# Stores of rotated queries and keys from GpSimd's DMA queue instead of SyncE's

## The chip, the cores and the metric

The kernel runs on one core of a Trainium2 chip. The metric is the device time of one launch in microseconds (us), the median of several runs. The core's engines are named TensorE (PE; PEld is its weight load), VectorE (DVE), ScalarE (ACT), GpSimd (POOL) and SyncE (SP); SyncE does no arithmetic here and only issues DMAs.

## The reference, cut to what matters

The reference is a transformer of two layers on 1024 main tokens and 256 context tokens, with a model dimension of 1024. Layer 0 has an attention mixer (a window attention with grouped keys and a differential attention over all tokens), layer 1 a gated linear attention; each is followed by a convolutional feed-forward network. Both are modulated by six vectors per layer, which are the products of a condition row with a large table. The part that matters here is the input of layer 0's attention: the normed tokens are projected to queries, keys and values, and the queries and keys of the main tokens are rotated by position.

```
aq, ak, av, bq, bk, bv = split(xn @ w_in)           # cn @ w_in for the context, not rotated
aq, ak, bq, bk = (apply_rope(t, cos, sin) for t in (aq, ak, bq, bk))
# apply_rope: x1, x2 = x[..., 0::2], x[..., 1::2]
#             even channels: x1 * c - x2 * s, odd channels: x1 * s + x2 * c
mod = silu(c) @ mod_w[layer] + mod_b[layer]          # six vectors: shift, scale, gate, twice
```

## The kernel before, in words

All operands are 32 bits wide. Every operand of a large product is split into a high part `hi` and a rest `lo`, and a product is three matmuls (hi by hi, hi by lo, lo by hi). `split` (L89) makes a pair of them: ScalarE copies the source to `hi`, then VectorE subtracts it from the source to give `lo`. Weights come in chunks of 512 KB through `load_w` (L95): a DMA into one of two buffers `wraw`, then a split into `whi` and `wlo` (three buffers each).

The stage of the change is `attn_in` (L292). It norms the tokens to `x1h` and `x1l`, and then runs fourteen projections (`part`, which calls `proj`, L103): each loads a weight chunk and multiplies it with all 1280 tokens, in two pieces of 512 columns and one of 256, eight chunks of the contraction deep and three matmuls each, into one of two PSUM buffers `big`. Six times two projections make a head pair (`pair`, L360): the even channels E of four heads and the odd ones O. VectorE multiplies the main tokens of both with cosine and sine (`ec`, `es`, `os`, `oc`, 1024 columns each), subtracts and adds, and the results are split into `shi` and `slo`, two buffers of each name; the 256 context columns are split straight from PSUM. Then the four results of the pair (hi and lo of the even and of the odd channels, 128 rows by 1280 columns, 640 KB each) are stored to a scratch in device memory: `qs` for the queries (pairs 0 to 3), `ks` for the keys (pairs 4 and 5). The scratch lies as [4 heads, 128 rows, 1280 tokens]; a store writes 32 rows of each head, `scr[:, r:r + 32, :]`. The two key heads of the window attention come from a projection of their own, in four stores of 320 KB (L405). The values are projected with the tokens as the stationary operand (`proj_tok`, L421, its matmuls at L434, 256 columns each), one half after the fourth pair and the other at the end of the stage.

In between, `some_mod` steps through the products of the condition rows with the modulation table, as work that VectorE does on the side: 48 blocks here, six after each pair and a few with the values. A block (`mod_block`, L247) is a DMA of 512 KB into one of two buffers `mraw` and two reducing products on VectorE (`junk` and `mraw`, with a short accumulator read).

The order of the work on each engine is laid down by the framework before the run: each engine has one list of instructions, and an instruction waits for semaphores at the head of its engine's list. In this stage no order is written out by hand. All DMAs of the stage, the loads of weights, table blocks and tables and also the stores, are issued from SyncE's list, by `dma` (L77). GpSimd's queue, by `dma2` (L80), is used for four DMAs late in the kernel; GpSimd does little else there (a few memsets). After the stage the attention reads the scratch back: ten keys of the context (`kc`), the queries (`q`, 120 DMAs) and ten keys of the main tokens (`km`), each load waiting for the stores that it reads from.

Of the kernel before, what the change touches and what calls it, by code (L numbers as in the profile page):

```python
# [9 lines left out]
F32 = mybir.dt.float32  # L10
# [8 lines left out]
P = 128  # L19
CC = 128                    # tokens of a chunk of the linear attention  # L20
KD = 8                      # chunks of the model dimension
NM = 1024                   # main tokens
NX = 256                    # context tokens
T = NM + NX
# [3 lines left out]
NB = 3                      # buffers of the norms  # L28
NFF = 22                    # chunks of the ffn dimension
# [5 lines left out]
class K:  # L35
    def __init__(self, nc, tc, io):
        self.nc, self.tc, self.io = nc, tc, io
        self.es = ExitStack()
        self.stacks = []
        self.urgent = False         # whether splits go before what was emitted earlier  # L40

    # ---------------------------------------------------------------- helpers
# [11 lines left out]
    def open_tmp(self, ny=2):  # L54
        """Room for the norms, on the right, until close_tmp."""
        self.es_tmp, self.ny = self.stack(), ny
        self.tmp = self.pool(self.es_tmp, "tmp", side="right")
# [22 lines left out]
    def dma2(self, out, in_):  # L80
        """On a queue of its own, for what would hold up the loads behind it."""
        return self.nc.gpsimd.dma_start(out, in_)

    def exp_tables(self, after):
        """Both Exp and Ln from one table set, until another function needs its own."""
        with self.tc.issue_after(after.ins):
            self.nc.scalar.preload_act_table_set("natural_log_exp_and_others")

    def split(self, hi, lo, src, urgent=False):  # L89
        """hi + lo = src: hi keeps 12 significant bits, lo the rest."""  # L90
        with self.tc.high_priority() if urgent else ExitStack():
            self.nc.scalar.copy(hi, src)  # L92
            self.tt(lo, src, hi.bitcast(F32), ALU.subtract)
# [8 lines left out]

    def proj(self, ps, w, xh, xl, tch, ks=range(KD)):  # L103
        """ps[:, t] += w^T x over the contraction chunks, weights stationary."""
        wh, wl = (a.rearrange("p (k n) -> p k n", k=KD) for a in w)
        for t0, n in tch:
            for k in ks:
                for j, (a, b) in enumerate(((wh, xh), (wh, xl), (wl, xh))):
                    self.nc.tensor.matmul(ps[:, t0:t0 + n], a[:, k, :], b(k, t0, n),  # L109
                                          start=(k == 0 and j == 0), stop=(k == KD - 1 and j == 2))  # L110

    def rstd_rows(self, hsrc, t0, n, on_pe=False):
        """1/sqrt(mean over the model dimension + eps), on every partition; on_pe: the squares are added up there."""
# [24 lines left out]
    def norm_mod(self, hsrc, xh, xl, t0, n, A, B, on_pe=False):  # L138
        """x = hsrc * rstd * A + B for tokens t0..t0+n, split in two."""
        y = self.rstd_rows(hsrc, t0, n, on_pe)  # L140
        for k in range(KD):
            self.norm_chunk(k, hsrc, xh, xl, t0, n, A, B, y)
# [8 lines left out]
    # ------------------------------------------------------------------ parts  # L151
    def setup(self):
# [23 lines left out]
        # per layer and norm: scale and shift of the normed rows, gate; [chunk, token kind]  # L176
# [4 lines left out]
        # scratch, in pieces that are written and read back each on its own  # L181
# [9 lines left out]
    def attn_consts(self, pool):  # L191
# [21 lines left out]
        # -lam  # L213
        self.stt(self.lam, ls[:, 1:2], -LAM_INIT, ls[:, 0:1], ALU.add, ALU.subtract)

    def mod_finish(self, l, j):
        """The j-th of the six vectors of layer l, once its products are there."""
# [15 lines left out]
    def mod_rows(self, pool, nv):  # L233
        """silu of the condition rows, on every partition."""
# [12 lines left out]
    def mod_block(self, pool, src, dst, rows):  # L247
        """dst[:, v] = block of the table, output rows on the partitions, times rows[v]."""
# [9 lines left out]
    def mod_first(self, pool, rows, load):  # L258
        """Shift and scale of the first norm: the one on the tensor engine, the other on the vector engine."""
# [24 lines left out]
    def mod_steps(self, todo, rows, pool):  # L284
        """The blocks of the vectors (l, j) of todo on the vector engine, one per step."""
# [8 lines left out]
    # -------------------------------------------------------- attention layer  # L294
    def attn_in(self, esv):
        nc, io = self.nc, self.io
        with ExitStack() as esx:
# [31 lines left out]
            with ExitStack() as es1:  # L329
# [27 lines left out]
                def pair(w0, scr):  # L357
                    """Four heads: their even channels, then their odd ones."""
                    def out(eo, t):
                        hi, lo = hl[eo]  # L360
                        self.split(hi[:, M], lo[:, M], t)
                        for half, y in ((0, hi), (1, lo)):
                            r = 64 * half + 32 * eo
                            self.dma(scr[:, r:r + 32, :], y.bitcast(F32))
# [26 lines left out]
                # the two key heads of the window attention: [even 0, even 1, odd 0, odd 1]  # L391
# [10 lines left out]
                for half, y in ((0, hi), (1, lo)):  # L402
                    for eo in range(2):
                        r = 64 * half + 32 * eo
                        self.dma(self.ks[2][:, r:r + 32, :], y[64 * eo:64 * eo + 64].bitcast(F32))  # L405
                some_mod(6)
                # values, token-major
# [13 lines left out]
    def proj_tok(self, srcs, fh, fl, dst, nblk):  # L421
        """256 columns, token-major: dst[b // per][:, b % per, :]."""
# [15 lines left out]
    def attn(self, fill, ahead):  # L438
        nc, io = self.nc, self.io
        with ExitStack() as es:  # L440
            es_k = es.enter_context(ExitStack())
            ap = self.pool(es, "attn")
            # keys: hi, lo on the rows; context and main tokens
# [29 lines left out]
            def scores(out, q, s, h, t0, n, mask=None):  # L473
                key = kc[h][:, t0 - NM:t0 - NM + n] if t0 >= NM else km[h][:, t0:t0 + n]
                nc.tensor.matmul(out, q[:, 0, s, :], key, start=True, stop=False)
                if mask is not None:
                    if n == 3 * P:
                        # the block in the middle is all in the window
# [8 lines left out]
            class Unit:  # L487
                """Shared by both kinds: the weights' transposes and their product with the values."""
# [29 lines left out]
            class UnitB(Unit):  # L518
# [20 lines left out]
                def w(self):  # L539
                    """p0 - lam (z0 / z1) p1, which still wants 1 / z0"""  # L540
# [83 lines left out]
            class CtxB(UnitB):  # L624
                """The two query blocks of the context; columns and sums by [block, map]."""
# [55 lines left out]
            class CtxA(UnitA):  # L681
                """Columns and sums by [block, head]."""
# [40 lines left out]
            def block_out(i, oc):  # L723
                """The block's outputs, transposed, to the scratch."""
# [31 lines left out]
            # A step takes one unit of either kind through its exponentials and  # L756
            # finishes the units of the step before.
# [61 lines left out]
    # ------------------------------------------------------ output projection  # L819
    def o_tiles(self, pool, name, n):  # L820
        """hi and lo of the mixer's outputs."""
# [4 lines left out]
    def halves_of(o, t0):  # L826
        """hi and lo as functions of chunk and tokens, which start at t0."""
        return [lambda k, a, b, t=t: t[k][:, a - t0:a - t0 + b] for t in o]

    def o_load(self, o, c, src, dma=None):  # L830
        """The split comes with the function that is returned."""
# [5 lines left out]
    def out_pass(self, wsrc, o, h, g, first=(), started=(), meanwhile={}):  # L837
        """h += gate * (w^T x) for the tokens of o, pairs of chunk and operands; started: sums that have the first pair."""
# [14 lines left out]
    # -------------------------------------------------------------------- ffn  # L853
    def ffn_first(self, l):
        """The first weights, ahead of the norm."""
# [6 lines left out]
    def ffn(self, l, fp, xh, xl, h, NT, first, in_order, last_norm, step, before_last, after_last, after):  # L862
# [8 lines left out]
        def load(group):  # L871
            """The group's chunks with their weights."""
            return [(self.load_w(io["ffn_down"][l, c]), a, b) for c, a, b in group]

        def down(group, order, after=None, urgent=False):
            """These chunks' part of the output, onto h."""
# [22 lines left out]
        # the first two projections begin while the last tokens are still being normed  # L899
# [51 lines left out]
    def body(self):  # L951
# [3 lines left out]
        with ExitStack() as esv:  # L955
# [6 lines left out]
            def begin():  # L962
                """The first output chunk of the projection, in between what ends the attention."""
# [19 lines left out]
        # output projection, norm2  # L983
# [30 lines left out]
        # ffn of layer 0, the condition's vectors of layer 1, then the first norm of layer 1  # L1014
# [79 lines left out]
        # gated linear attention  # L1094
# [42 lines left out]
    def gla_open(self, st):  # L1137
        """What the linear attention keeps throughout, at the right's bottom."""
# [7 lines left out]
        # the second gate product, its hi and lo parts stacked on the rows  # L1146
        self.w2 = [gp.tile([P, 512], F32R, name=f"w2s{d}") for d in range(2)]

    def gla_rst(self, rst, w, xh, xl, tch, off):
        """Low-rank gate rows: hi, lo, hi on rows 0, 32, 64 (+16) of rst[direction]; ones for the bias."""  # L1150
# [14 lines left out]
    def gla_ctx(self, st):  # L1165
        """The context's final states, either direction."""
# [44 lines left out]
    def gla_gates(self, pool, rst, h, d, n, L, b):  # L1211
        """b: running sums of 16 log a over each chunk (inclusive); L: the summands."""
# [17 lines left out]
    def gla_khat(self, k, b, be, n, m):  # L1230
        """k times the decay to the chunk's end (forward) and to its start (backward)."""
# [17 lines left out]
    def gla_decay(self, pool, b, bb, nch):  # L1249
        """exp of the chunk sums, [P, 2, nch]"""  # L1250
# [5 lines left out]
    def gla_update(self, dst, src, dec, kt, v):  # L1256
        """dst = dec * src + k^T v"""
# [7 lines left out]
    def gla(self, st):  # L1265
        nc, io = self.nc, self.io
        ch = self.ch
        with ExitStack() as es:
# [16 lines left out]
            for h in range(4):  # L1285
# [7 lines left out]
                # running sums: X inclusive (forward), exclusive (backward); I inclusive  # L1293
# [5 lines left out]
                # within a chunk: scores[s, t], from the diagonal outwards  # L1299
# [7 lines left out]
                for lev in range(7):  # L1307
# [5 lines left out]
                    # F[0]: decays that go with the keys, F[1]: with the queries  # L1313
# [17 lines left out]
                # across chunks  # L1331
# [13 lines left out]
                # states before each chunk, in either direction  # L1345
# [8 lines left out]
                # gate of the output  # L1354
# [8 lines left out]
                if h == 3:  # L1363
                    # the output projection's operands of the first tokens
# [12 lines left out]
                # outputs, token-major, normed over the head's columns  # L1377
# [35 lines left out]
# --------------------------------------------------------------------- layout  # L1413
def _chunks(w):
    """[1024, N] -> [N/128, 128 (rows in a chunk), 8 (row chunks) * 128]"""
# [4 lines left out]
def _cols(v):  # L1420
    """[..., 1024] -> [128, ..., 8]"""
# [4 lines left out]
def _wide(w):  # L1426
    """[1024, N] -> [N/256 * 2, 128, 4 * 256]: row chunks 0..3, then 4..7, of each 256 columns"""
# [5 lines left out]
def layout(x, c, ctx, c_ctx, mod_w, mod_b, norm1_g, norm2_g, attn_w_in, attn_w_out, attn_sink,  # L1433
# [17 lines left out]
    # rope tables: row p holds the angle of channel pair p % 32  # L1451
# [7 lines left out]
    # query and key columns: of four heads the even channels, then the odd ones  # L1459
# [14 lines left out]
    # window mask for the blocks before, at and after the query block  # L1474
# [50 lines left out]
```

## Time and profile before

| | us |
|---|---|
| median of the runs (3) | 3219.08 |
| lowest and highest run | 3217.68, 3223.64 |
| profiled execution: its span, first to last instruction | 3216.0 |
| busy in that span: TensorE | 3048.9 (95%) |
| busy: VectorE | 2026.6 (63%) |
| busy: ScalarE | 1142.7 (36%) |
| busy: GpSimd | 10.9 (0%) |

The page gives the span of the profiled execution and no other time for it; the runs' times contain what lies around the span as well. The shares are those of the whole kernel, an average over stages with different limits: what a change in one stage is worth has to be read in that stage. "Granted clock" is the share of TensorE's full speed; in the whole span it is 0.980. Waits are put down to the one of an instruction's semaphores that came last.

### The profile page before, as it was taken

To read this page: it belongs to the slowest core of one execution; us is meant where nothing else is said; L and a number is where in the kernel's file an instruction comes from. 1 tells how busy PE (TensorE), PEld (TensorE's weight loads), DVE (VectorE), ACT (ScalarE), POOL (GpSimd) and SP (SyncE) were. 2 spreads that over 40 slices of the span, in tenths; PEclk is the share of its full clock that TensorE was granted. 3 is DMA by queue.
4 is the path that set the end of the run, shared out by engine and by line. 5 is a ranking of instruction groups with operands and counts; after the bars stand their busy time and mean duration, and the time that the engine had idled before them with its cause. 6 is when DMAs were issued, how large, how long until landed. Compare 5 with 4: busy or idle time off the path is not lost. (4 is left out here: it accounts for less than half of the span.)

```text
span 3216.0 us, 40083 instructions
## 1 busy us (share of the span) xinstructions
PE 3048.9 (95%) x16390; PEld 2569.6 (80%) x16390; DVE 2026.6 (63%) x3124; ACT 1142.7 (36%) x1884; POOL 10.9 (0%) x22
## 2 busy tenths in 40 slices
PE   8768669999999999999999999999999999999998
PEld 4667569999887888888888878888877888888887
DVE  7566467888578744545455597688776554555546
ACT  5111147777443222222222264445354222221223
POOL 0000000000000000000000000000000000000000
PEclk9889789999999999999999999999999999999999
DMA  6434492221425311111111141111142111111111
GB/s 219 158 135 155 147 226 82 60 60 37 168 72 165 123 35 38 40 40 40 33 40 39 35 150 55 43 40 45 42 158 73 53 40 53 52 47 40 58 48 59
DMA packets 127831, 257.41 MB, mean 80 GB/s; under 512 B 11324, under 2 KB 70844, under 8 KB 127648
## 3 DMA queue, kind: packets, MB, share of 16 engines
q1 hardware_dynamic: 125600, 251.71, 23.9%
q8 instruction: 129, 2.11, 0.3%
q10 hardware_dynamic: 1728, 2.10, 0.2%
q0 software_dynamic: 320, 1.05, 0.1%
q14 instruction: 54, 0.44, 0.0%
HBM read 219.42 MB, written 35.39 MB: 79 GB/s over the span
## 5 line engine op out<-in xcount | busy, mean ns | idle before, releaser
L92 ACT CAST whi<-wraw 128x1024 fp32r<-128x1024 f32 x218 | 226.2, 1048 | 1202.3 <-PE big L109 641.9
L72 DVE TENSOR_TENSOR wlo<-wraw,whi 128x1024 fp32r<-128x1024 f32 x218 | 264.2, 1220 | 477.7 <-ACT whi L92 476.1
L109 PE MATMUL big<-x2h,whi 128*128 128x512 f32 (+1 forms) x1056 | 377.4, 357 | 1.8 <-ACT crow L75 1.2
L109 PE MATMUL big<-x2l,whi 128*128 128x512 f32 (+1 forms) x1056 | 377.0, 357 | 0.4 <-DVE x2l L69 0.3
L109 PE MATMUL big<-x2h,wlo 128*128 128x512 f32 (+1 forms) x1056 | 377.1, 357 | 0.0
L887 PE MATMUL sm<-gh,whi 128*128 128x512 f32 (+1 forms) x904 | 332.5, 368 | 3.0 <-DVE h L69 1.9
L887 PE MATMUL sm<-gl,whi 128*128 128x512 f32 (+1 forms) x904 | 329.3, 364 | 0.2 <-DVE gl L72 0.2
L887 PE MATMUL sm<-gh,wlo 128*128 128x512 f32 (+1 forms) x904 | 328.6, 364 | 0.0
L69 DVE SCALAR_TENSOR_TENSOR cv<-big,cw,cv 128x1023 f32<-128x1023 f32 (+1 forms) x264 | 267.1, 1012 | 21.0 <-ACT cv L75 17.7
L109 PE MATMUL big<-x4l,whi 128*128 128x512 f32 x704 | 277.7, 394 | 0.9 <-DVE x4l L69 0.9
L109 PE MATMUL big<-x4h,whi 128*128 128x512 f32 x704 | 276.7, 393 | 1.9 <-ACT x4h L75 1.9
L109 PE MATMUL big<-x4h,wlo 128*128 128x512 f32 x704 | 274.0, 389 | 0.0
L69 DVE SCALAR_TENSOR_TENSOR h<-sm,G,h 128x512 f32<-128x512 f32 (+1 forms) x280 | 179.8, 656 | 90.6 <-PE sm L887 89.9
L109 PEld LDWEIGHTS big<-x2h,whi 128*128 128x128 f32 x1056 | 198.8, 188 | 34.1 <-ACT crow L75 2.0
L109 PEld LDWEIGHTS big<-x2l,whi 128*128 128x128 f32 x1056 | 198.7, 188 | 32.5 <-DVE x2l L69 1.1
L109 PEld LDWEIGHTS big<-x2h,wlo 128*128 128x128 f32 x1056 | 198.6, 188 | 31.2
L887 PEld LDWEIGHTS sm<-gh,whi 128*128 128x128 f32 x904 | 170.3, 188 | 41.7 <-DVE h L69 7.4
L69 DVE SCALAR_TENSOR_TENSOR hh<-sm,G,hh 128x512 f32<-128x512 f32 (+1 forms) x192 | 137.5, 726 | 87.4 <-PE sm L887 87.1
L887 PEld LDWEIGHTS sm<-gh,wlo 128*128 128x128 f32 x904 | 170.3, 188 | 27.5 <-issue 0.2
L887 PEld LDWEIGHTS sm<-gl,whi 128*128 128x128 f32 x904 | 170.4, 189 | 26.6 <-DVE gl L72 0.6
L75 ACT ACTIVATE cv<-big,cb,cw 128x1024 f32<-128x1024 f32 (+1 forms) x132 | 130.6, 990 | 125.7 <-DVE cv L69 125.1
L109 PE MATMUL big<-x1h,whi 128*128 128x512 f32 (+1 forms) x336 | 125.3, 375 | 48.9 <-DVE slo L72 47.1
(348 smaller groups left out, 6141.4 us busy)
## 6 DMA issues: line engine op xcount, KB each, us to landing
mraw<-in_mod_wt_dram SPq DMA_DIRECT2D x88, 512.0 KB
wraw<-in_ffn_up_dram SPq DMA_DIRECT2D x88, 512.0 KB
wraw<-in_ffn_down_dram SPq DMA_DIRECT2D x44, 512.0 KB
q<-qs SPq DMA_DIRECT2D x40, 256.0 KB
q<-qs SPq DMA_DIRECT2D x80, 128.0 KB
wraw<-in_attn_w_out_dram SPq DMA_DIRECT2D x16, 512.0 KB
wraw<-in_gla_w_v_dram SPq DMA_DIRECT2D x16, 512.0 KB
wraw<-in_gla_w_out_dram SPq DMA_DIRECT2D x16, 512.0 KB
```

Source lines behind the costliest of these rows:

```text
L69: return self.nc.vector.scalar_tensor_tensor(out=out, in0=in0, scalar=scalar, in1=in1, op0=op0, op1=op1)
L72: return self.nc.vector.tensor_tensor(out=out, in0=a, in1=b, op=op)
L75: return self.nc.scalar.activation(out=out, in_=in_, func=func, **kw)
L92: self.nc.scalar.copy(hi, src)
L109: self.nc.tensor.matmul(ps[:, t0:t0 + n], a[:, k, :], b(k, t0, n), start=(k == 0 and j == 0), stop=(k == KD - 1 and j == 2))
L887: nc.tensor.matmul(o, w[:, d * P:(d + 1) * P], x[:, t0:t0 + n], start=(i == 0), stop=(i == 3 * len(group) - 1))
```

## The change

The 28 stores of rotated and split queries and keys to the scratch are issued from GpSimd's queue (`dma2`) instead of SyncE's (`dma`). Their sizes, sources, destinations and number stay, and so do all loads. The diff also drops comments and docstrings, line by line, so that line numbers stay; two lines of code differ:

```diff
@@ pair(w0, scr), out(eo, t) @@
                         self.split(hi[:, M], lo[:, M], t)
                         for half, y in ((0, hi), (1, lo)):
                             r = 64 * half + 32 * eo
-                            self.dma(scr[:, r:r + 32, :], y.bitcast(F32))
+                            self.dma2(scr[:, r:r + 32, :], y.bitcast(F32))
@@ the two key heads of the window attention @@
                 for half, y in ((0, hi), (1, lo)):
                     for eo in range(2):
                         r = 64 * half + 32 * eo
-                        self.dma(self.ks[2][:, r:r + 32, :], y[64 * eo:64 * eo + 64].bitcast(F32))
+                        self.dma2(self.ks[2][:, r:r + 32, :], y[64 * eo:64 * eo + 64].bitcast(F32))
```

## Rows read from the trace of the kernel before

**Rows 1.** The page: span.

```profile
span 3216.0 us, 40083 instructions
```

**Rows 2.** Timeline of SyncE: start, us, instruction; first store of some pairs.

```profile
88.32 0.69 SPq L78 DMA_DIRECT2D qs<-shi  x1
...
231.02 0.52 SPq L78 DMA_DIRECT2D qs<-shi  x1
...
308.27 0.52 SPq L78 DMA_DIRECT2D ks<-shi  x1
...
354.03 0.53 SPq L78 DMA_DIRECT2D ks<-shi  x1
```

**Rows 3.** Busy time by stretch, 60 to 428 us, sum of seven stretches.

```profile
sum 368.00, PE 267.41 PEld 233.03 DVE 215.59 ACT 54.59 POOL 0.00; mean PE 38.20 PEld 33.29 DVE 30.80 ACT 7.80 POOL 0.00
```

**Rows 4.** Waits of TensorE, 60 to 428 us: total us, times, longest.

```profile
PE big L109 <- DVE slo L72: 47.1, 7, 14.0
PE big L434 <- DVE slo L72: 16.5, 2, 15.9
PE big L434 <- DVE wlo L72: 14.5, 1, 14.5
PE big L109 <- DVE wlo L72: 12.7, 1, 12.7
```

**Rows 5.** Waits of VectorE, 60 to 428 us.

```profile
DVE junk L255 <- DMA mraw<-in_mod_wt_dram: 138.6, 17, 22.2
```

**Rows 6.** Timeline of VectorE, 148 to 171 us; in brackets idle before, releaser.

```profile
148.53 1.21 DVE L72 TENSOR_TENSOR es<-big,sin 128x1024 f32<-128x1024 f32 x1
149.66 1.21 DVE L72 TENSOR_TENSOR wlo<-wraw,whi 128x1024 fp32r<-128x1024 f32 x1
169.51 1.22 DVE L255 CUSTOM_DVE_ANT_0 junk<-mraw,crow 128x1024 bf16<-128x1024 f32 x1 [18.64 <-DMA mraw<-in_mod_wt_dram]
...
170.66 0.42 DVE L72 TENSOR_TENSOR slo<-big,shi 128x256 fp32r<-128x256 f32 x1
```

**Rows 7.** Timeline of SyncE, 142 to 158 us: DMA issues.

```profile
142.85 3.21 SPq L78 DMA_DIRECT2D qs<-slo  x1
146.16 7.43 SPq L78 DMA_DIRECT2D mraw<-in_mod_wt_dram  x2
153.64 4.74 SPq L78 DMA_DIRECT2D wraw<-in_w_v_dram  x2
```

**Rows 8.** DMA view, 139 to 172 us in 40 slices: busy share in tenths, GB/s.

```profile
DMA  0222132222222222479699838952222222222221
GB/s 0 50 50 62 74 107 68 99 99 99 99 93 99 112 112 99 125 215 400 243 389 395 359 149 191 385 223 106 106 112 99 106 99 81 84 104 104 104 109 79
```

**Rows 9.** DMA view of the whole span: one group of stores, KB each.

```profile
qs<-shi SPq DMA_DIRECT2D x8, 640.0 KB
```

**Rows 10.** Timeline of GpSimd, one of its four DMAs, and their landing (tile og).

```profile
2385.45 0.55 POOL L82 DMA_DIRECT2D oraw<-og  x1 [0.90 <-PE big L109]
DMA to landing us min/median/max: 2.3/3.3/7.2
```

**Rows 11.** Timeline of TensorE, 367 us: steps of 512 and of 256 columns.

```profile
367.17 0.40 PE L109 MATMUL big<-x1h,wlo 128*128 128x512 f32 x1
367.40 0.29 PE L109 MATMUL big<-x1h,whi 128*128 128x256 f32 x1
367.52 0.28 PE L109 MATMUL big<-x1l,whi 128*128 128x256 f32 x1
```

**Rows 12.** Timeline of VectorE, 419 to 426 us: one block of the table, two blocks on

```profile
419.77 1.23 DVE L255 CUSTOM_DVE_ANT_0 junk<-mraw,crow 128x1024 bf16<-128x1024 f32 x1 [0.98 <-DMA mraw<-in_mod_wt_dram]
...
425.74 1.23 DVE L255 CUSTOM_DVE_ANT_0 junk<-mraw,crow 128x1024 bf16<-128x1024 f32 x1 [0.91 <-DMA mraw<-in_mod_wt_dram]
```

**Rows 13.** Timeline of TensorE, 415 to 447 us: stage's last, attention's first.

```profile
418.78 0.28 PE L434 MATMUL big<-whi,x1l 128*128 128x256 f32 x1
432.69 0.55 PE L475 MATMUL big<-kc,q 128*128 128x256 f32 x1 [13.63 <-DMA q<-qs]
```

## The prediction

> **What bounds the kernel now.** I read the page first: the span is 3216.0 us [rows 1]. Then I looked for the stretch that the moved stores live in. The queue of SyncE shows the first of the four stores of each head pair starting at 88.32, 231.02, 308.27 and 354.03 us [rows 2]; the first three pairs are 142.7 us apart in all (47.6 each), the fourth, with one projection of the values in between, 77.3 us, the last 45.8 us. So this is the input stage of the attention, from about 60 to 428 us, and only there can the change act directly. The table by stretch says that TensorE is busy for 267.4 of these 368 us [rows 3]: 100 us are idle, in a kernel whose TensorE is otherwise the bound. The waits of TensorE name VectorE in four lines, 47.1 + 16.5 + 14.5 + 12.7 = 90.8 us [rows 4]. The waits of VectorE in turn name one thing: 138.6 us for blocks of the modulation table (mraw), 17 times, up to 22.2 us at a time [rows 5].
>
> One such wait, followed down: VectorE finishes a weight split at 150.9 us and then stands still for 18.64 us, until 169.51, for a block of mraw; behind it in its order is the split of the projection's context columns (slo from big), which is what frees the sum that TensorE needs [rows 6]. The loads it waits for were issued long before: SyncE issued the last of the four stores at 142.85, then two mraw blocks (from 146.16) and two weight blocks (from 153.64) [rows 7]. What holds them is seen in the DMA slices from 139 to 172 us, 0.825 us each: the busy share is 0.2 for the first 13 us, while only the stores move, at about 100 GB/s; then it is 0.5 to 0.9 for some 8 us, when the loads run; then it is 0.2 again until 171 us [rows 8]. A share of 0.2 to 0.25 is four of 16 engines. A pair has four stores of 640 KB [rows 9], 2.62 MB; at 105 GB/s that is 25 us, from 140 to 165. The loads finish on twelve engines in 8 us, and their share on the four, a quarter of 2.1 MB at 105 GB/s, 5 us, comes behind the stores: 165 + 5 = 170, where the wait ends. So the loads are late because on four engines they stand behind the stores.
>
> **The change, part by part.** It moves 28 stores (24 of 640 KB, 4 of 320 KB) to GpSimd's queue. Nothing is added or removed in the arithmetic. SyncE loses their issue and their waits: in one pair 3.3 us from the last store's issue to the next load's [rows 7]; taken alone this is hidden by the backlog above, and I count it at nothing beside it. GpSimd has nothing to do in this stretch (POOL busy 0 [rows 3]), so nothing queues behind a store that waits there for its split. Its price for a DMA stands in the only four that it issues today: 0.55 us busy, 1.45 us from one to the next, 2.3 to 7.2 us to landing for 256 KB [rows 10]. Four stores are issued in about 6 us of a pair of 30; it is hidden, and would cost only if it delayed the reuse of the split buffers by the next pair's first split, some 10 us after the stores.
>
> What the stores cost the loads then is not in the trace, since no store of this shape leaves from GpSimd. The one end: they spread over all engines. A pair moves 2.62 MB of stores and eight blocks of 512 KB, 6.8 MB in all; at 300 GB/s, which the mixed slices of [rows 8] reach (215 to 400), that is 23 us, less than either compute engine needs. The other end: they stay on the same four engines, only no longer ahead of the loads; then these four carry 25 us of stores and a quarter of 4.2 MB of loads, 10 us, 35 us a pair. I take the first, as the rows of GpSimd's own DMAs show 256 KB landed in as little as 2.3 us, which is 110 GB/s with the whole of issue and receipt in it, so that the moving alone was well above the 105 GB/s of four engines.
>
> With timely loads a pair costs:
> - TensorE: matmuls of 512 columns follow each other by 0.23 us, those of 256 by 0.12 [rows 11]. A projection has 48 and 24, 13.9 us; a pair 27.8; the values' projection has 240 of the short ones, 28.8.
> - VectorE: ten instructions of 1024 columns (six of the rotation, two splits, two weight splits) by 1.13 us [rows 6] are 11.3, two short splits 0.8, together 12.1. Six mraw blocks: at the stage's end, with no store in the way, two blocks take 5.97 us including a wait of 0.9 [rows 12], so six take 17.9. Some of these waits go where a block was fetched during the rotation; I take 17.3. Sum 29.4.
>
> So VectorE is next late, by little. I take 32 us a pair, 2.6 above this floor for the order between the two (VectorE's last blocks delay a freed sum). Between the pairs' stores: 5 x 32 + 28.8 = 189 us against 354.03 - 88.32 = 265.7, a gain of 77. After the last pair two projections, the transposes and the values' second half: from 354.03 to the last matmul of the stage at 418.78 [rows 13] 64.8 us pass; unhindered it is 6.4 to 13.9 for the first (TensorE has begun it before the last stores leave, or not), 13.9 for the second, 1 for the transposes and 28.8, about 54. A gain of 11. What follows, the start of the attention with its own loads, shifts as it is; I count no gain there. Sum: 88 us, so a span of 3216.0 - 88 = 3128. The median of the runs, 3219.08, is 3.1 above the profiled span; I take that as what lies around it and predict 3131.
>
> The bounds of this case: at the floor of 29.4 a pair, 5 x 29.4 + 28.8 = 176, a gain of 89, and 15 behind it (6.4 taken for the first projection), 104: 3115. At 36 a pair, 57 + 8 = 65: 3154.
>
> **The rivals.**
>
> *The stores keep their four engines.* Loads then pass them, but the four engines are busy for 35 us a pair, and the stores, stretched by the loads, hold the split buffers; the wait of VectorE for mraw is replaced by the one for the landing of a store. With 3 to 6 us of order on top a pair takes 38 to 41: 5 x 39.5 + 28.8 = 226, a gain of 40, and some 8 in the tail: 3171, from 3155 to 3190. For it: the shape of the transfer does not change, and the rows show this shape on four engines. Against it: the rate of GpSimd's DMAs above. [...]
>
> *Nothing to speak of.* The wait moves on: the two mraw buffers or the order that is laid down anew for the changed queues keep VectorE as late as now. For it: 0.9 us of wait for every second block stays without any store [rows 12]. Against: that is 3 us a pair, not the 18 to 22 of today. 3200 to 3222.
>
> *Slower: GpSimd can't issue fast enough.* The stores land so late that the next pair's splits wait for the buffers, and VectorE with them. The price: it decides from the point where four stores take longer than today's pair, 46 us, 11.5 us each, eight times the 1.45 us of [rows 10]; at 15 us each a pair takes 60, six pairs lose 84: 3303. For it: VectorE is busy nearly throughout a pair then, and the landing of 256 KB varied from 2.3 to 7.2 us. [...] Against: the factor of eight.
>
> **How the numbers follow.** Chances: the forecast 0.66 (3115 to 3154), four engines 0.20 (3155 to 3190), nothing to speak of 0.09, slower 0.05. The range from 3112 to 3182 holds nearly all of the first and most of the second, 0.8. Faster or slower by over 0.2% is 6.4 us, about what a measurement here can tell from no change. Faster takes the first two and half of the third, 0.91; within it 0.05; slower 0.04.
>
> **What would show it.** Right: the waits of VectorE for mraw fall from 138.6 to some 20 to 35 us, those of TensorE for VectorE from 90.8 below 25; pairs' stores on POOL about 32 us apart; the last matmul of the values near 331 us; no long plateau at a share of 0.2 that ends with a wait for mraw. Four engines: the plateau stays, VectorE waits for stores to land. Slower: issues on POOL many us apart. The forecast is wrong if the pairs' spacing falls and the stage's end does not, or if the attention behind it gives the gain back: its first score product starts 13.9 us after the stage's last matmul today [rows 13], and that gap should keep its length.

## The result and the profile after

The changed kernel takes 3164.11 us (median of four runs, 3162.18 to 3169.22) against 3218.38 us (four runs, 3216.29 to 3223.64): a ratio of 0.9833, interval 0.9819 to 0.9847. It is 54 us faster, of the 88 that were forecast. The time lies inside the range of the prediction and above its likeliest case (3115 to 3154).

The page gives the span and the busy times; those of TensorE and VectorE are the same as before to 0.3 us, so the gain is idle time.

```profile
span 3164.1 us, 40097 instructions
PE 3048.6 (96%) x16390; PEld 2570.0 (81%) x16390; DVE 2026.3 (64%) x3124; ACT 1142.1 (36%) x1884; POOL 29.9 (1%) x50
```

The timeline of GpSimd from 84 to 330 us, the first of the four stores of each of the six pairs and the rest of the first four; it answers to [rows 2].

```profile
87.35 0.86 POOL L82 DMA_DIRECT2D qs<-shi  x1 [86.89 <-ACT shi L92]
88.88 0.71 POOL L82 DMA_DIRECT2D qs<-slo  x1 [0.67 <-DVE slo L72]
89.58 0.68 POOL L82 DMA_DIRECT2D qs<-shi  x1
91.14 0.69 POOL L82 DMA_DIRECT2D qs<-slo  x1 [0.88 <-DVE slo L72]
132.36 0.68 POOL L82 DMA_DIRECT2D qs<-shi  x1 [40.53 <-ACT shi L92]
...
173.62 0.68 POOL L82 DMA_DIRECT2D qs<-shi  x1 [36.78 <-ACT shi L92]
...
214.12 0.68 POOL L82 DMA_DIRECT2D qs<-shi  x1 [36.03 <-ACT shi L92]
...
284.33 0.68 POOL L82 DMA_DIRECT2D ks<-shi  x1 [65.72 <-ACT shi L92]
...
323.37 0.68 POOL L82 DMA_DIRECT2D ks<-shi  x1 [34.56 <-ACT shi L92]
```

Pairs are 45.0, 41.3, 40.5 and 39.0 us apart, not 32, and 70.2 with the values in between. In all 323.37 - 87.35 = 236.0 us against 265.7: a gain of 29.7 where 77 were expected.

The waits of TensorE and VectorE in the same stage, now 60 to 380 us (total us, times, longest); they answer to [rows 4, 5].

```profile
PE big L109 <- DVE slo L72: 28.0, 7, 8.2
PE big L434 <- DVE slo L72: 13.4, 2, 10.1
PE big L434 <- DVE wlo L72: 7.9, 2, 7.7
PE big L109 <- DVE wlo L72: 6.0, 1, 6.0
DVE junk L255 <- DMA mraw<-in_mod_wt_dram: 92.8, 23, 13.7
```

TensorE's waits for VectorE fell from 90.8 to 55.3 us, VectorE's for the table from 138.6 to 92.8. It is the same chain of waits as before, with shorter links. A wait of TensorE can cost more than its length: after one of 6.4 us, up to 158.54, the granted clock is 0.50 until 163.80, and matmuls of 512 columns follow each other by 0.43 us there instead of 0.23.

The DMA view from 132 to 173 us, one pair, in 40 slices of 1.025 us; it answers to [rows 8]. The queue rows give packets, MB and the share of 16 engines (q0 is GpSimd's, q1 SyncE's).

```profile
DMA  0329799699699898799631100002938987850000
GB/s 0 36 45 176 214 227 165 154 215 245 225 334 295 304 293 297 237 234 340 260 141 73 55 33 28 0 0 52 308 152 256 316 280 200 276 208 0 0 0 0
q0 software_dynamic: 2112, 2.63, 29.0%
q1 hardware_dynamic: 1152, 4.19, 28.9%
```

The view of the tile mraw in the same stretch, six blocks:

```profile
DMA to landing us min/median/max: 3.1/9.0/17.3
```

The plateau at 0.2 is gone: the stores are on all 16 engines (at the peak some 16 of their packets of 5120 bytes move at once in the trace, mostly four before). But the engines are then 0.6 to 0.9 busy for some 17 us and move no more than 150 to 340 GB/s. The stores alone take 0.29 x 41 x 16 = 190 engine-us for 2.63 MB; before, four engines for some 25 us, 100. So the stores moved to four times the engines and cost almost twice the engine time, and a table block that goes out among them lands after up to 17.3 us.

The end of the stage and the start of the attention: TensorE, then SyncE's issues of after, SyncE's of before, and VectorE's of before. The TensorE rows answer to [rows 13].

```profile
380.44 0.28 PE L434 MATMUL big<-whi,x1l 128*128 128x256 f32 x1
380.56 0.28 PE L475 MATMUL big<-kc,q 128*128 128x256 f32 x1
...
368.82 0.33 SPq L78 DMA_DIRECT2D mraw<-in_mod_wt_dram  x1
...
369.77 4.91 SPq L78 DMA_DIRECT2D kc<-ks  x10
```

```profile
422.30 0.33 SPq L78 DMA_DIRECT2D mraw<-in_mod_wt_dram  x1
...
423.16 4.70 SPq L78 DMA_DIRECT2D kc<-ks  x10
...
413.88 1.22 DVE L255 CUSTOM_DVE_ANT_0 junk<-mraw,crow 128x1024 bf16<-128x1024 f32 x1 [20.83 <-DMA mraw<-in_mod_wt_dram]
```

The gap of 13.9 us between the two matmuls shrank to 0.1. Before, VectorE stood for 20.8 us at the stage's end for a late block; so it freed the buffers late, SyncE issued the last block only at 422.30, after TensorE's last matmul (418.78), and the attention's first loads stand behind that block in SyncE's list. Now they go out at 369.77, 11 us ahead of the stage's end. The whole gain up to the attention's first score product, 432.69 - 380.56 = 52.1 us, is then: first stores 1.0 earlier, pairs 29.7, tail after the last pair 64.8 - 57.1 = 7.7, start of the attention 13.8. The spans differ by 51.9, so almost nothing is given back later.

### The profile page after: what moved, and what is told of

Its sections match the earlier page's. It is cut to its first block, busy times and chain, and to the rows that moved or that the text cites. A ratio compares the mean times of both kernels' runs of the same rounds, so it can differ in the third digit from the quotient of the medians.

```text
span 3164.1 us, 40097 instructions
## 1 busy us (share of the span) xinstructions
PE 3048.6 (96%) x16390; PEld 2570.0 (81%) x16390; DVE 2026.3 (64%) x3124; ACT 1142.1 (36%) x1884; POOL 29.9 (1%) x50
## 2 busy tenths in 40 slices
DMA packets 139184, 257.46 MB, mean 81 GB/s; under 512 B 22676, under 2 KB 82196, under 8 KB 139000
## 3 DMA queue, kind: packets, MB, share of 16 engines
q1 hardware_dynamic: 122168, 234.67, 22.7%
## 5 line engine op out<-in xcount | busy, mean ns | idle before, releaser
L109 PEld LDWEIGHTS big<-x4h,whi 128*128 128x128 f32 x704 | 132.2, 188 | 34.1 <-ACT x4h L75 3.2
```

## The experiments

The theory after the result: what makes the loads late is how long, and on which engines, the stores hold the DMA engines; from GpSimd they use all 16 but crowd each other. Its rivals: four engines after all, with other packets between; the order laid down for the new queue; or a limit on writing as such. Beside these runs the kernel before had medians of 3218.7 to 3221.6 us.

**Stores alone (e5).** The network is replaced by groups of four stores, each group after the one before has landed:

```diff
+            for j in range(m):
+                q(s[:, 32 * j:32 * j + 32, :], src[j])
...
+        gate(); rows4(sy)
+        gate(); rows4(po)
+        gate(); rows4(ac)
...
+                for h in range(4):
+                    q(s[h, 32 * j:32 * j + 32, :], src[j][32 * h:32 * h + 32])
...
+                q(s[j], src[j])
```

> The whole network is left out; only groups of stores run, one group behind the other, with nothing beside them, and the output is filled with ones. Four stores of the kernel's form: from SyncE 25 us on four engines (share 0.25, 105 GB/s); from ScalarE the same four engines, 25 us; from GpSimd all 16 engines, four to a store. Theory 'crowded stores' (four stores on 16 engines slow each other, 5120-byte packets of 400 to 540 ns where one alone takes 196): 16 to 18 us at about 155 GB/s with no load near, while one store alone from GpSimd takes 7 us and two 7 to 9. Rival 'the loads beside them slow the stores': four from GpSimd alone take 7 to 9 us at 300 GB/s or more. If crowded: a limit on writing to device memory as such expects 155 GB/s for the head-by-head and the contiguous form too; a limit from the four stores reading the same rows of SBUF expects 300 GB/s and more for the head-by-head form (all engines on different rows) and no gain from a scratch for each store; a limit from the addresses in the scratch expects a gain from a scratch for each store.

The busy time by stretch, one stretch for each group, from where its first packets move (some 1.2 us behind the first issue) to its landing: us, busy times of VectorE and GpSimd, granted clock, share of 16 DMA engines, GB/s. In this order: the kernel's form from SyncE, GpSimd, ScalarE; one and two such stores from GpSimd; head by head from GpSimd; one whole contiguous block for each store from GpSimd.

```profile
9.20:36.30 27.10, 1.24 (x6) 0.00 (x0) 1.00 0.25 97
39.00:57.80 18.80, 1.24 (x6) 1.48 (x3) 1.00 0.69 140
60.00:88.00 28.00, 1.24 (x6) 0.00 (x0) 1.00 0.24 94
90.50:99.20 8.70, 0.00 (x0) 0.00 (x0) 1.00 0.25 76
102.30:115.30 13.00, 0.41 (x2) 0.15 (x1) 1.00 0.42 101
118.10:128.50 10.40, 1.24 (x6) 6.73 (x14) 1.00 0.84 252
...
143.40:150.20 6.80, 1.24 (x6) 1.11 (x3) 1.00 0.97 386
```

From SyncE or ScalarE the form keeps to a quarter of the engines (0.25 and 0.24) for 27 to 28 us. From GpSimd one store takes a quarter, two take 0.42, four 0.69, yet four need 18.8 us. The shares grow with the number of stores, so from GpSimd several at once are not held to one quarter. As engine time (us x share x 16) a store costs 27 from SyncE, 35 alone from GpSimd, 44 of two and 52 of four; why the one alone costs more than from SyncE stays open. The same bytes as contiguous blocks take 6.8 us at 386 GB/s: writing as such is no limit. One store and two were slower than expected (8.7 and 13.0 us for 7 and 7 to 9): already two disturb each other.

**No stores but the first pair's (e4).** The five other pairs and the window keys store nothing; all reads take the first scratch.

```diff
-                            self.dma2(scr[:, r:r + 32, :], y.bitcast(F32))
+                            if w0 == 0:
+                                self.dma2(scr[:, r:r + 32, :], y.bitcast(F32))
```

> The stores of all pairs but the first, and those of the window's keys, are left out, and all queries and keys are read from the first pair's scratch. Theory 'the stores still delay the loads': pairs 29 to 33 us apart (39 to 41 now), VectorE's waits for mraw in the stage under 40 us (92.8 now), time 3110 to 3130. Rival 'the loads' own buffers and order hold them': pairs 38 to 41 us apart, waits over 70 us, time 3150 to 3165.

One run: 3108.43 us, just under the theory's range. The casts of the odd sum, which mark the pairs, are 28.6, 28.7, 59.5 and 27.0 us apart from the second pair on. VectorE's wait for the table is left with this row of its waits from 60 to 300 us:

```profile
DVE junk L255 <- DMA mraw<-in_mod_wt_dram: 30.4, 15, 13.5
```

Up to the end of the stage it is 34.2 us, against 92.8 in the changed kernel. So the stores are what makes the loads late, and without them a pair takes a little less than the floor of the forecast, 29.4 us.

**ScalarE's queue (e1).** The loads' queue is freed of the stores too, but the form keeps to four engines' worth there (share 0.24 in e5).

```diff
-                            self.dma2(scr[:, r:r + 32, :], y.bitcast(F32))
+                            nc.scalar.dma_start(scr[:, r:r + 32, :], y.bitcast(F32))
```

> The 28 stores from ScalarE's queue. Their engines are the four that SyncE's stores take (share 0.25 while only stores run), but they don't stand in SyncE's queue. Theory 'leaving the loads' queue is what helps, spreading adds little': 3155 to 3175, as the change. Rival 'the spread over 16 engines is what helps': 3185 to 3215, with a plateau at 0.25 and loads that end only with it. In both ScalarE loses some us a pair, as its queue stands at a store that waits for VectorE.

3191.26 us (3186.3 to 3193.46), ratio 0.9908, interval 0.9891 to 0.9924. The DMA view from 137 to 178 us (q10 is ScalarE's queue):

```profile
DMA  2226979587222222222972798722862884222223
q10 hardware_dynamic: 583, 2.90, 18.9%
```

ScalarE's list near the end of the stage, and one of TensorE's waits:

```profile
357.62 15.05 ACTq L405 DMA_DIRECT2D ks<-slo  x2
...
PE sm L414 <- ACT shi L410: 15.5, 1, 15.5
```

The plateau at 0.2 is there again, as in [rows 8], and the gain is half of the change's, 27 of 54 us. VectorE's wait for the table is 81.0 us in 28 pieces, none over 8.1; it also waits 11.3 us for stores to land. So a queue of their own lets the loads past the stores even where these keep to a quarter of the engines. That the other half goes with the spread over 16 doesn't follow. From the first pair's stores to the last pair's it is 242.2 us, against 236.0 in the change and 265.7 before: in the pairs the change is only some 6 us better than the queue alone on four engines, 30 and 24 us. TensorE's waits for VectorE come to 56.8 us, as in the change (55.3). The largest piece of the difference is one wait: ScalarE, whose list now holds the stores, takes 15.05 us to issue two of the window's, and TensorE stands 15.5 us for the copy behind them. Whether the work in ScalarE's list or the backlog on few engines makes that issue so long was not separated. The time lies in the range of the theory that held the spread to matter, but mostly for this other reason.

**Which rows are read together (e8).** Again groups of stores alone, and groups with eight table blocks behind them.

```diff
+        for block in (lambda j: j, lambda j: 0):
+            gate()
+            for j in range(4):
+                s, = scr(1, (4, 9, 4 * T))
+                po(s[:, 0:8, :], wide[j][32 * block(j):32 * block(j) + 32])
...
+                q(s[:, 32 * j:32 * j + 32, :].rearrange("h p t -> p h t"), src[j])
...
+            for k in range(8):
+                sy(w[k], io["mod_wt"][k])
```

> Again only groups of stores, then stores beside eight loads of 512 KB; the network is left out and the output is filled with a constant. (a) the kernel's form from GpSimd again 18 to 19 us. (b) heads 33 rows apart and a scratch for each store: 18 us if the device memory's addresses don't matter, under 12 if they do. (c) and (d) move 655 KB a store on four engines: if engines that read the same rows of SBUF at the same time hold each other up, (d), all four from the same 32 rows, takes 15 to 20 us or more and (c), each from rows of its own, 7 to 8; if SBUF has no part in it, both take the same. (e), (f) rows dealt in turn to the four heads, one DMA over 16 engines: 6.6 us from either queue. (g) eight loads behind four stores on SyncE's queue end 35 us after the start (27 of stores, then a quarter of the loads, 10); (h) with the stores from GpSimd 26 to 30 us, as both share all engines; (i) with the stores of (e) 17 to 19 us.

Stretches as before: four stores from four different blocks of 32 rows of the on-chip memory; all from one block; the kernel's rows dealt to the heads in turn, from GpSimd and from SyncE; then with eight loads: kernel's form from SyncE, the same from GpSimd, dealt rows from GpSimd.

```profile
84.50:97.30 12.80, 1.56 (x8) 1.20 (x3) 1.00 0.82 205
100.40:121.90 21.50, 1.17 (x7) 1.25 (x3) 1.00 0.81 122
124.50:131.20 6.70, 1.61 (x9) 1.11 (x3) 1.00 0.98 391
134.30:141.70 7.40, 1.78 (x10) 0.00 (x0) 1.00 0.88 355
146.30:183.90 37.60, 5.84 (x30) 0.00 (x0) 1.00 0.50 181
189.60:219.00 29.40, 5.12 (x28) 1.54 (x3) 1.00 0.81 232
224.50:242.60 18.10, 5.21 (x29) 1.06 (x2) 1.00 0.98 377
```

Stores that read the same rows at once hold each other up (21.5 us), but four different blocks, expected at 7 to 8 us, still took 12.8. A scratch for each store, with its heads 33 rows apart, changed nothing (19.1 us, 18.6 without), so it is not the addresses written. A pair's stores and loads together take 37.6, 29.4 and 18.1 us in the three forms. Dealt means that row p of a store goes to head p mod 4: the outermost count is then 32 instead of 4, and the share of the 16 engines is 0.98 from GpSimd and 0.88 from SyncE, where the kernel's form had 0.69 and 0.25. Which engine reads which rows no view shows.

**Which blocks disturb each other (e10).** The 12.8 us asked for this one: stores of 32 rows of 20480 bytes that differ only in their first row.

```diff
+        for rows in ((0,), (0, 0), (0, 32), (0, 64), (0, 96), (0, 32, 64, 96), (0, 64, 0, 64), (0, 32, 0, 32), (0, 0, 0, 0), (0, 32), (0, 64)):
+            gate()
+            for j, r in enumerate(rows):
+                s, = scr(1, (4, 9, 4 * T))
+                po(s[:, 0:8, :], wide[j][r:r + 32])
```

> The network is left out; groups of stores from GpSimd run alone, each store 640 KB from 32 rows of 20480 bytes of the on-chip memory, on four DMA engines of eight rows each. The groups differ only in the first row of each store: 0; 0 and 0; 0 and 32; 0 and 64; 0 and 96; 0, 32, 64, 96; 0, 64, 0, 64; 0, 32, 0, 32; four times 0; and once more 0 and 32, 0 and 64. One store alone should take some 7 to 9 us. Theory 'rows': stores hold each other up only where they read the same rows. Then 0 and 0 takes 12 to 14 us and the three other pairs 8 to 10; 0, 32, 0, 32 takes as long as 0, 64, 0, 64. Theory 'rows 32 apart count as the same': 0 and 32 takes as long as 0 and 0, 12 to 14 us, while 0 and 64 and 0 and 96 take 8 to 10; 0, 32, 0, 32 takes as long as four times 0, 20 to 22 us, and 0, 64, 0, 64 some 12 to 13, as the four different blocks did (12.8). [...] Rival 'any neighbour': stores on neighbouring engines slow each other whatever they read; then all pairs take the same 12 to 14 us.

Stretches from the first issue to the end of VectorE's last wait for a landing, in the order of the diff (the two repeats agreed, 12.4 and 9.0; counted in this way the 12.8 and 21.5 of e8 are 14.3 and 22.7):

```profile
31.70:40.75 9.05, 1.86 (x14) 0.71 (x1) 1.00 0.19 73
43.03:55.74 12.71, 2.11 (x14) 1.15 (x2) 1.00 0.39 103
57.81:70.34 12.53, 2.13 (x15) 1.16 (x2) 1.00 0.40 105
72.41:81.50 9.09, 2.13 (x15) 1.16 (x2) 1.00 0.37 144
83.56:92.59 9.03, 2.14 (x15) 1.16 (x2) 1.00 0.37 145
94.66:107.39 12.73, 1.80 (x12) 2.32 (x4) 1.00 0.76 206
109.97:122.60 12.63, 2.20 (x14) 2.32 (x4) 1.00 0.74 208
124.86:146.87 22.01, 1.81 (x13) 2.32 (x4) 1.00 0.71 119
149.27:171.07 21.80, 1.80 (x12) 2.32 (x4) 1.00 0.71 120
```

Rows 0 and 32 disturb each other as much as 0 and 0 do (12.5 and 12.7 us); 64 or 96 rows away, two stores take no longer than one (9.1, 9.0). Four stores on 0, 32, 0, 32 take as long as four times 0 (22.0 and 21.8). So in these runs rows 32 apart count as the same, rows 64 apart don't, and the rival of any neighbour, with 12 to 14 us for all pairs, falls. It fits the 12.8 us: of four blocks 0 and 32 are such a pair, 64 and 96 lie as far apart, and the four take 12.7 us here, as long as one such pair. A store of the kernel's form reads all four blocks, so four at once can meet on the same rows or on rows 32 apart. That this gives the direction of the 18.8 us is the author's estimate; in which order the engines go over the rows, which would set the number, was not measured. From SyncE a store of the same rows costs no more engine time than a dealt one (27 and 26 us); so rows 32 apart in one store need not slow it.

**One store for each head, from GpSimd (e2).** Alone, a pair's stores in this form kept the 16 engines 0.84 busy, in 10.4 us (e5); 104 DMAs instead of 28.

```diff
-                            self.dma2(scr[:, r:r + 32, :], y.bitcast(F32))
+                            for h in range(4):
+                                self.dma2(scr[h, r:r + 32, :], y[32 * h:32 * h + 32].bitcast(F32))
```

> Each store is cut into one DMA for each head (32 rows, all 16 engines), from GpSimd: 104 DMAs in place of 28. Alone these took 10.3 us for a pair, in place of 18.7. Theory 'time on the engines': 3115 to 3145. Rival 'any stores beside the loads': 3150 to 3170.

3137.26 us (3135.66 to 3139.43), ratio 0.9739, interval 0.9724 to 0.9753: in the range of the theory of time on the engines and 27 us below the change at the same queue; the form, the number of DMAs and the lists laid down for them are what differs. VectorE waits 34.4 us for the table in place of 92.8, and once 24.0 us for a weight copy of ScalarE's, which is a matter of the order. The attention's gap is not always closed: here its first score product starts 9.3 us after the stage's last matmul (348.06 and 338.75).

**Rows dealt to the heads, three queues (e6, e7, e9).** The columns of the projections are permuted beforehand, so that row p of a result belongs to head p mod 4; the cosine and sine tables follow (the window keys get their own, two loads more); the scratch is laid out as before. The store is then one DMA, in the form that had a share of 0.98 and 0.88 in e8. The queue differs: GpSimd (e6), SyncE (e7), ScalarE (e9). Of e7:

```diff
-                            self.dma2(scr[:, r:r + 32, :], y.bitcast(F32))
+                            self.dma(scr[:, r:r + 32, :].rearrange("h p t -> p h t"), y.bitcast(F32))
...
-                cols.append(m[:, 4 * g:4 * g + 4, eo::2].reshape(1024, P))
+                cols.append(m[:, 4 * g:4 * g + 4, eo::2].transpose(0, 2, 1).reshape(1024, P))
...
+        d[name] = con(np.repeat(x, 4, axis=0))
```

> The channels of the queries and keys are dealt in turn to the four heads (columns of the weights and rows of the tables permuted in the layout, two small tables more to load), so that each store of 640 KB goes out on 16 engines as one DMA, from GpSimd's queue. Theory 'what is left of the delay is the long time that the stores hold the engines': four stores take 7 us in place of 18 or more, pairs 30 to 33 us apart, VectorE's waits for mraw 35 to 50 us, 3108 to 3130. Rival 'any stores beside the loads delay them as much, since bytes and engines are the same': pairs 38 to 41 us, 3150 to 3170.

> The same permuted channels, but with the stores on SyncE's queue as before the change. Theory 'the stores' time on the engines is the cause, the queue only its carrier': 3108 to 3140, within 15 us of the permuted version from GpSimd. Rival 'it is the queue: loads behind stores that wait for splits': 3175 to 3215, near the kernel before.

> The permuted channels, one DMA of 16 engines a store, from ScalarE's queue. Open after the last runs: from SyncE's queue this form gave 3099 us with 17.8 us of waits for mraw, from GpSimd's 3109 with 37.7. Theory 'stores of a queue of their own share the engines with the loads packet by packet, so each load lands later than when it stands ahead of them': 3104 to 3116, waits 30 to 40 us. Rival 'GpSimd's way of issuing costs the difference': 3097 to 3103, waits 15 to 22 us.

| | us (lowest to highest) | ratio, interval |
|---|---|---|
| e6, GpSimd | 3109.14 (3105.13 to 3110.95) | 0.9649, 0.9635 to 0.9664 |
| e7, SyncE | 3099.36 (3097.87 to 3100.16) | 0.9619, 0.9603 to 0.9635 |
| e9, ScalarE | 3109.66 (3105.56 to 3112.26) | 0.9653, 0.9639 to 0.9668 |

All three are far below the change, and the best has the stores back on SyncE, below the 3108 to 3140 that its theory expected. Its waits from 60 to 300 us, and the sum of its busy times over 89 to 300 us in six stretches:

```profile
DVE junk L255 <- DMA mraw<-in_mod_wt_dram: 16.9, 13, 3.2
PE big L109 <- DVE slo L72: 4.1, 1, 4.1
sum 211.00, PE 211.00 PEld 185.21 DVE 188.33 ACT 36.62 POOL 0.00; mean PE 35.17 PEld 30.87 DVE 31.39 ACT 6.10 POOL 0.00
```

From the first pair's stores on, TensorE has not a hole in this stage. From a store's issue to its landing 3.8 to 5.3 us pass (medians by group); in the changed kernel it is 11.5 to 17.4. Up to its last matmul the stage is 66 us shorter than the changed kernel's: 51 are waits of TensorE (55.3 and 4.1 us), 15 are the same matmuls at a higher clock (busy 265.4 us at a mean granted clock of 0.90, and 250.4 us at 0.99). That settles the main question: with the queue undone and the form mended, 122 us are gained; with the form kept and the queue changed, 54. Why the other two queues lie 10 us behind stays open: 7 to 8 of them are there at the stage's last matmul (321.2 and 321.9 against 314.3), and VectorE waits longer for the table (34.2 us in e6, 25.3 in e9, both up to 310 us). The time of e9 fits the theory of engines shared by queues; its waits (25.3 us) fall short of the 30 to 40 that this theory expected.

**One store for each head, from SyncE (e3).** As e2, with SyncE's queue.

```diff
-                            self.dma2(scr[:, r:r + 32, :], y.bitcast(F32))
+                            for h in range(4):
+                                self.dma(scr[h, r:r + 32, :], y[32 * h:32 * h + 32].bitcast(F32))
```

> Each store cut into one DMA for each head (32 rows, all 16 engines), from SyncE's queue as before the change; from GpSimd the same cut gave 3137 us. Theory 'time on the engines, the queue matters little, and standing behind the loads even helps': 3115 to 3137. Rival 'a queue of their own is needed for stores this long (10 us a pair alone)': 3140 to 3175.

3161.85 us (3158.51 to 3164.79), ratio 0.982, interval 0.9803 to 0.9836: slower than the theory expected and inside the range of its rival, that stores this long need a queue of their own. The order that the framework laid down for SyncE puts a weight load behind the stores of two pairs: no weight block is issued between 98 and 169 us, and TensorE then waits 35.6 us at once. So the run says something of an order, and can't be counted for the rival; e7 has its stores on the same queue.

## Why the prediction was right, and where it was not

*What bounds the stage: right.* Late loads, VectorE, TensorE in that order; taking away the stores alone (e4) takes most of the waits away (TensorE's for VectorE fall to 11.8 us).

*GpSimd's own cost: right.* An issue takes 0.68 us, four go out in 4.5 us (predicted: about 6), and none comes late. The rival "slower" had its price from 11.5 us a store on; nothing of the kind is seen.

*"They spread over all engines", 32 us a pair, a gain of 77: the step that failed, in its size.* They do spread, but the argument for their speed came from stores of another form, 256 KB that landed in 2.3 us [rows 10]. The forecast took it that 16 engines move these stores at the rate of mixed slices, 23 us of transfer a pair. Alone they take 18.8 us and not 7, beside the loads 29.4 and not 23 (e5, e8). That stores of rows 32 apart slow each other (12.5 us for two, 9.1 for two that are 64 apart) would give the direction of this (e10), not its size. The 29.4 us still fit into 32; in e8 eight loads go out at once, whereas the kernel has two buffers for the table, and SyncE issues a block when VectorE has freed one, into the crowd. That this makes 39 to 45 us out of 29.4 is a reading of the trace; more buffers were not tried.

*The floor of 29.4 us a pair: near, a little high.* 27.0 to 28.7 in e4, 27.2 to 32.9 in e7. It counted a wait of 0.9 us for every second block, and had VectorE next late; in e7 TensorE is busy for all of the 211 us from the first pair's stores on, VectorE for 188.

*The tail, 11 us: nearly.* 7.7, by the same late blocks.

*"The start of the attention shifts as it is": wrong.* 13.8 us came from there, a quarter of the whole gain. The loads of the attention stand in SyncE's list behind the stage's last table block; what made VectorE late made them late too. It was to be seen in the trace of before: VectorE's wait of 20.8 us and SyncE's issue behind the stage's end. The 3.1 us around the span, a median less the span of one run, are in a single run 1.8 (3165.92 against 3164.1).

So two errors stood against each other: 47 us too much for the pairs and 3 for the tail, 14 too little at the attention's start and 1 before the first pair; some 36 in all before rounding, of which the time around the span and the step from this run to the median take 3 back: 3164 against 3131.

*The signs put down ahead.* Waits of 20 to 35 us, pairs 32 us apart and no plateau belong together in e6 (34.2 up to 310 us and 37.7 in the whole stage, 8.3 of TensorE, pairs 31 to 33 apart, 3109 us): the kernel that was forecast is the one with the dealt rows. Of the change only the plateau's end came true.

*The rivals.* "The stores keep their four engines" came near the measured pairs (38 to 41 us against 39 to 45) and a time of 3155 to 3190, but not its sign: no plateau, and VectorE waits only 2.8 us for a store's landing. Its time came out by another mechanism, which was no rival of mine: 16 engines that are crowded for some 17 us a pair, in place of four that are held for 25. The rival as it was put, four engines and a queue of their own, is e1: pairs of 37.0 to 47.0 us, the plateau, 11.3 us of waits for landings, and 3191 us. So a second issuer was worth something here: ScalarE's queue gave 27 us and GpSimd's 54, as stores that fill a quarter of the engines stood ahead of loads in one queue. How much of either gain comes from the lists that were laid down anew for SyncE and VectorE was not separated; the lists of TensorE and ScalarE are the same before and after.

## What to carry to other kernels

Before a DMA is moved to another queue, look at how many engines its form holds, and for how long: a plateau of the busy share at a quarter (0.25), with loads behind it, pointed to the form here. Mend that first: with the rows dealt, at a share of 0.88, the same bytes took 7.4 us in place of 27 on the old queue, and the kernel gained 122 us there, where the new queue alone gave 54. And follow a late load past the end of its stage: what stood behind it in the same list came late as well, and was worth 13.8 us here.

## What was not expected of the hardware

- Stores that read rows 32 apart of the on-chip memory at once slowed each other as if they read the same rows (12.5 and 12.7 us for two stores); 64 apart they didn't (9.1, and 9.05 for one alone).
- More engines cost more engine time here: a store of 640 KB took 27 engine-us on SyncE's four engines, 52 on GpSimd's sixteen beside three others, 26 with the rows dealt to the heads.
- A store of this form from GpSimd brings tiny packets with it: the whole kernel moves 22676 packets under 512 bytes, before 11324, some 400 for each of the 28 stores. In the pair from 132 to 173 us the trace has 1600 of them in GpSimd's queue, of 4 bytes each, beside 512 packets of 5120 bytes. They take 7 to 9 ns each, for the pair 13 of the 190 us of engine time, so they are not what makes the form dear.
